# A 90 degree rotation of an 8192 x 8192 fp32 matrix: macro tiles of 512 rows with 4 MB stores in place of 1024 rows with 2 MB stores

## The chip, the cores and the metric

The kernel runs on one core of a Trainium2 chip. The metric is the time of one execution on the device in microseconds (us). The kernel before has a median of 1267.76 us over two runs (1267.45 and 1268.06).

## The reference

The input `x` is an 8192 x 8192 fp32 matrix (268.44 MB), `k` is 1, and the output has the same size:

```python
def reference(x, k):
    return np.rot90(x, k)
```

With k = 1 the output is `out[i, j] = x[j, 8191 - i]`: a transpose, with the order of the output's rows reversed. Every element is read once and written once, and nothing is computed on it.

## The kernel before

**Tiling.** The matrix is cut into macro tiles of R = 1024 rows by W = 4096 columns. There are 16 of them; `macro_tiles` cuts the last in two of 512 rows (`LAST`). A macro tile goes through four stages, and `load` and `store` are its two halves.

**Load.** A macro tile's rows come in row tiles of 128 (the partitions), 4096 columns each: one DMA of 2 MB, 16 KB to a partition, issued on SP's queue (line 102) into a buffer `a` (two of them; in the first macro tile some of the loads borrow an output buffer). VectorE (DVE, line 108) then copies the row tile in eight chunks `ar` of 512 columns and reverses the order of the columns in each block of 128. Chunks come from a ring of 63 buffers of 2 KB, in the order (row tile, chunk). A buffer comes free when TensorE (PE) has made the last transpose that reads it, and DVE waits for that. SP issues a load as soon as the `a` buffer that it writes has been copied out.

**Transposes.** PE turns each 128 x 128 block (line 148) and writes it into a PSUM tile `pt` of 128 x 2048 fp32, of which there are two. A PSUM tile takes 16 transposes.

**Evacuation and store.** ScalarE (ACT, line 169) copies a PSUM tile into the output buffer `ot`. There are three output buffers of 16 KB to a partition (F = 4096 elements), and each takes two PSUM tiles. ACT then issues the store on its own queue (line 177): 2 MB, 128 partitions of 16 KB, written to four output rows' pieces of 4 KB (1024 elements, the macro tile's rows). A macro tile has eight such stores. In the first macro tile two of them, and the last store of all, are issued as two stores of 1 MB (`S = PW`), which read 8 KB from a partition. The two macro tiles of 512 rows at the end write runs of 2 KB: their stores have 16 KB to a partition, in eight runs. `whole_reads` rewrites the read side of each DMA, so that what is contiguous in a partition is one read.

**Order.** Within an engine the order is that of the program. Load DMAs wait on SP only for DVE. Store DMAs wait on ACT only for ACT's copies. The two DMA queues, q1 (loads) and q10 (stores), share the core's 16 DMA engines. Transposes of a macro tile's first output are issued as each row tile comes in (`if i == 0 and ...`); all others follow once the whole macro tile is loaded. The next macro tile's loads go on meanwhile, as far as the chunk ring and the two `a` buffers allow. For the last two macro tiles the generators interleave loads and stores by hand.

Of the kernel before, what the change touches and what calls it, by code (L numbers as in the profile page):

```python
# [2 lines left out]

# [5 lines left out]

P = 128  # L10

R = 1024
RT = R // P
LAST = [4, 4]
W = 4096
CH = 512
F = 4096  # L20
FP = 2048


def whole_reads(nc):

    for fn in nc.m.functions:
        for block in fn.blocks:
            for n, ins in enumerate(block.instructions):
                if not isinstance(ins, mybir.InstDMACopy):
                    continue
                src = ins.ins[0]
                ap = [list(d) for d in src.ap]
                if len(ap) == 3 and ap[2][0] == 1 and ap[1][0] == ap[2][1]:
                    ap = [ap[0], [1, 1], [1, ap[1][1] * ap[2][1]]]
                    block.instructions[n] = copy.replace(  # L40
                        ins,
                        ins=[copy.replace(src, ap=ap)],
                        ant_dge_precooked=False,
                    )


def macro_tiles(N, M):

    tiles = [(r0, RT, c0) for r0 in range(0, N, R) for c0 in range(0, M, W)]
    r0, _, c0 = tiles.pop()  # L50
    for n in LAST:
        tiles.append((r0, n, c0))
        r0 += n * P
    return tiles


@with_exitstack
def kernel(
    ctx: ExitStack,
    tc: tile.TileContext,  # L60
    x: bass.AP,
    k: bass.AP,
    out: bass.AP,
):
    nc = tc.nc
    assert k == 1, f"only k=1 supported, got {k}"
    nc.at_finalize(whole_reads)

    N, M = x.shape
    dt = x.dtype  # L70

    consts = ctx.enter_context(tc.tile_pool(name="consts", bufs=1))
    ident = consts.tile([P, P], dt)
    make_identity(nc, ident)

    a_pool = ctx.enter_context(tc.tile_pool(name="a_pool", bufs=2))
    r_pool = ctx.enter_context(tc.tile_pool(name="r_pool", bufs=63))
    o_pool = ctx.enter_context(tc.tile_pool(name="o_pool", bufs=3))
    psum_pool = ctx.enter_context(
        tc.tile_pool(name="psum", bufs=2, space=bass.MemoryType.PSUM)  # L80
    )

    loads = 0

    def load(r0, rt, c0):

        nonlocal loads
        chunks = {}
        for t in range(rt):


            if loads < RT and loads % 5 >= 2:
                a = o_pool.tile([P, W], dt, tag="o")
            else:
                a = a_pool.tile([P, W], dt, tag="a")  # L100
            loads += 1
            nc.sync.dma_start(  # L102
                out=a[:], in_=x[r0 + t * P : r0 + (t + 1) * P, c0 : c0 + W]
            )
            yield chunks
            for j in range(W // CH):
                ar = r_pool.tile([P, CH // P, P], dt, tag="ar")
                nc.vector.tensor_copy(  # L108
                    out=ar[:],
                    in_=a[:, j * CH : (j + 1) * CH].rearrange(  # L110
                        "r (b m) -> r b m", m=P
                    )[:, :, ::-1],
                )
                chunks[t, j] = ar
            yield chunks

    def store(r0, rt, c0, chunks, end):

        rows = rt * P
        PW = 1
        while 2 * PW * rows <= FP:
            PW *= 2
        G = PW
        while 2 * G * rows <= F:
            G *= 2
        for i, g0 in enumerate(range(0, W // P, G)):  # L130
            if end and i % 2 == 0:
                ot = a_pool.tile([P, F], dt, tag="a")
            else:
                ot = o_pool.tile([P, F], dt, tag="o")
            o = ot[:, : G * rows].rearrange("m (g f) -> m g f", g=G)

            lead = r0 == 0 and c0 == 0 and i in (4, 6)
            S = PW if lead or (end and r0 + rows == N and g0 + G == W // P) else G  # L140


            ps = {}

            def transposes(t, ws):
                for w in ws:
                    g = g0 + w
                    nc.tensor.transpose(  # L148
                        ps[w // PW][:, PW - 1 - w % PW, t * P : (t + 1) * P],
                        chunks[t, g * P // CH][:, g % (CH // P), :],  # L150
                        ident,
                    )

            def psum_tile(h):
                pt = psum_pool.tile([P, FP], mybir.dt.float32, tag="ps")
                ps[h] = pt[:, : PW * rows].rearrange("m (g f) -> m g f", g=PW)

            if i == 0 and (rt == RT or r0 + rows < N):
                for h in range(G // PW):
                    psum_tile(h)  # L160
                for t in range(rt):
                    transposes(t, range(G))
            for h in range(0, G, PW):
                if h // PW not in ps:
                    psum_tile(h // PW)
                    for w in range(h, h + PW):
                        for t in range(rt):
                            transposes(t, [w])
                nc.scalar.copy(o[:, G - PW - h : G - h, :], ps[h // PW])  # L169

                done = h + PW
                if done % S == 0:
                    top = M - c0 - (g0 + done) * P
                    dst = out[top : top + S * P, r0 : r0 + rows].rearrange(
                        "(g m) f -> m g f", g=S
                    )
                    nc.scalar.dma_start(  # L177
                        out=dst, in_=o[:, G - done : G - done + S, :]
                    )
            yield  # L180

    tiles = macro_tiles(N, M)
    *most, before_last, last = tiles
    for m in most:
        *_, chunks = load(*m)
        for _ in store(*m, chunks, False):
            pass


    *_, chunks = load(*before_last)  # L190
    outputs = store(*before_last, chunks, True)
    rows = load(*last)
    for _ in range(2 * last[1] - 1):
        next(rows)
    next(outputs)
    chunks = next(rows)
    for _ in outputs:
        pass
    for _ in store(*last, chunks, True):
        pass  # L200


# [1 line left out]
_INS = ['x', 'k']  # L204
_OUTS = [((8192, 8192), 'float32')]

_NUMBERS = {'k': 1}


# [26 lines left out]
```

## Time and profile before

| What | Value |
|---|---|
| median of two runs | 1267.76 us |
| the profiled execution's span | 1266.1 us |
| PE busy | 718.2 us (57%), 4096 transposes |
| ACT busy | 466.7 us (37%), 256 copies of 1869 ns |
| DVE busy | 355.4 us (28%), 1024 copies of 421 ns |
| DMA | 537.55 MB, mean 425 GB/s |
| loads | 128 of 2 MB, median 16.8 us from issue to landing |
| stores | 125 of 2 MB, median 25.5 us; 6 of 1 MB, 27.3 us |
| TensorE clock, mean granted | 0.762 |

The page gives the profiled execution's own span; the median of the runs is 1.7 us above it. "Busy" is the time in which an engine had an instruction at work. A queue's line gives its packets, its megabytes and the time that its packets took as a share of the 16 DMA engines' time: two queues at 50% each leave no DMA engine free. A packet here is what is read from or written to one partition in one go; each DMA adds 16 very small ones (the lines' "under 512 B").

### The profile page before, as it was taken

Reading aid. Unit: us, or ns where it says so; the run is one execution under the profiler, and the core shown is the slowest. Engines: PE = TensorE matmul, PEld = TensorE weight load, DVE = VectorE, ACT = ScalarE, POOL = GpSimd, SP = SyncE. Lnnn points to the kernel's source line nnn. Section 1 sums busy time; section 2 is a strip of 40 time slices with the busy share of each in tenths; the row PEclk is TensorE's granted clock in tenths of the full one; section 3 lists DMA queues with packets and bytes.
Section 4 is the critical chain, followed back from the end, with each engine's and each line's share of the span. In section 5 each row is a group of like instructions: output and inputs, shape, how many; then the busy total and the mean of one; then the engine's idle time right before and its main releaser. Section 6 shows DMA issues by size and latency. Waiting matters only on the chain.

```text
span 1266.1 us, 10392 instructions
## 1 busy us (share of the span) xinstructions
PE 718.2 (57%) x4096; PEld 678.6 (54%) x4096; DVE 355.4 (28%) x1024; ACT 466.7 (37%) x257; POOL 0.7 (0%) x6
## 2 busy tenths in 40 slices
PE   1554565556656665556555665555655656556673
PEld 1543455555555555456554655555655655556562
DVE  4423223222232223222232223322232222322210
ACT  0432433433333333343334333343333433343363
POOL 0000000000000000000000000000000000000000
PEclk9977877777776777867778678677686686776797
DMA  9999999999999999999999999999999999999997
GB/s 399 426 428 430 428 429 427 430 429 429 429 429 429 430 428 427 430 429 430 428 430 428 429 429 428 430 428 428 430 430 428 429 429 428 428 428 428 427 399 328
DMA packets 37345, 537.55 MB, mean 425 GB/s; under 512 B 4144, under 2 KB 4144, under 8 KB 4144
## 3 DMA queue, kind: packets, MB, share of 16 engines
q10 hardware_dynamic: 18864, 268.44, 50.0%
q1 hardware_dynamic: 18432, 268.44, 49.7%
q8 instruction: 32, 0.52, 0.2%
q14 instruction: 17, 0.14, 0.0%
HBM read 268.44 MB, written 268.44 MB: 424 GB/s over the span
## 4 chain that ended last, share of the span: by engine, by line
DMA 82%; ACT 14%; PE 1%; issue 1%; ACTq 1%; DVE 0%; SPq 0%
DMA out_dram<-ot 79%; ACT ot L169 14%; DMA a<-in_x_dram 3%; PE pt L148 1%; ACTq L177 0%; DVE ar L108 0%; ACTq L169 0%; SPq L102 0%
## 5 line engine op out<-in xcount | busy, mean ns | idle before, releaser
L148 PE MATMUL pt<-ident,ar 128*128 128x128 f32 x4096 | 718.2, 356 | 528.0 <-ACT ot L169 487.6
L148 PEld LDWEIGHTS pt<-ident,ar 128*128 128x128 f32 x4096 | 678.6, 191 | 567.4 <-ACT ot L169 521.4
L169 ACT COPY ot<-pt 128x2048 f32<-128x2048 f32 x256 | 465.4, 1869 | 756.7 <-DMA out_dram<-ot 727.0
L108 DVE COPY ar<-a 128x512 f32<-128x512 f32 x1024 | 355.4, 421 | 861.1 <-DMA a<-in_x_dram 524.0
L169 ACT ACT_TABLE_LOAD x1 | 1.3, 1283 | 25.5 <-DVE ar L108 25.5
masks.py:199 POOL TENSOR_SCALAR_AFFINE_SELECT ident<-ident 128x128 f32<-128x128 f32 x1 | 0.3, 292 | 0.1
masks.py:197 POOL MEMSET ident<- 128x128 f32 x1 | 0.2, 204 | 0.3 <-POOLq L217 0.3
L217 POOL MEMSET const-bfloat16-1.0<- 128x1 bf16 x1 | 0.1, 102 | 0.0
L217 POOL MEMSET const-uint8-127<- 128x1 uint8 x1 | 0.1, 102 | 0.0
L217 POOL MEMSET const-float32-0.0<- 128x1 f32 x1 | 0.1, 99 | 0.2 <-issue 0.2
L217 POOL MEMSET const-float32-1.0<- 128x1 f32 x1 | 0.1, 99 | 0.0
## 6 DMA issues: line engine op xcount, KB each, us to landing
a<-in_x_dram SPq DMA_DIRECT2D x128, 2048.0 KB, 16.8
out_dram<-ot ACTq DMA_DIRECT2D x125, 2048.0 KB, 25.5
out_dram<-ot ACTq DMA_DIRECT2D x6, 1024.0 KB, 27.3
```

Of the source, the lines that this page charges most:

```text
L108: nc.vector.tensor_copy(out=ar[:], in_=a[:, j * CH : (j + 1) * CH].rearrange("r (b m) -> r b m", m=P)[:, :, ::-1],)
L148: nc.tensor.transpose(ps[w // PW][:, PW - 1 - w % PW, t * P : (t + 1) * P], chunks[t, g * P // CH][:, g % (CH // P), :], ident,)
L169: nc.scalar.copy(o[:, G - PW - h : G - h, :], ps[h // PW])
L217: nc = _bacc.Bacc("TRN2", target_bir_lowering=False, num_devices=1)
```

## The change

The macro tile has 512 rows instead of 1024, so there are 32 of them, each with four loads. F becomes 8192: an output buffer has 32 KB to a partition and takes four PSUM tiles, so a macro tile has two stores of 4 MB. Each reads 32 KB from a partition and writes it in 16 runs of 2 KB. The number of output buffers stays three. The chunk ring has 36 buffers instead of 63; a macro tile has 32 chunks. The special cases go: no loads into output buffers at the start, no split stores, no half macro tile at the end, no transposes ahead of the macro tile's last load other than by the plain loop order, and no interleaving of the last two macro tiles.

```diff
-R = 1024
+R = 512
 RT = R // P
-LAST = [4, 4]
 W = 4096
 CH = 512
-F = 4096
+F = 8192
 FP = 2048
...
-    r_pool = ctx.enter_context(tc.tile_pool(name="r_pool", bufs=63))
+    r_pool = ctx.enter_context(tc.tile_pool(name="r_pool", bufs=36))
...
+    PW = FP // R
+    G = F // R
+    for r0, c0 in [(r0, c0) for r0 in range(0, N, R) for c0 in range(0, M, W)]:
         chunks = {}
+        for t in range(RT):
+            a = a_pool.tile([P, W], dt, tag="a")
+            nc.sync.dma_start(out=a[:], in_=x[r0 + t * P : r0 + (t + 1) * P, c0 : c0 + W])
             for j in range(W // CH):
                 ar = r_pool.tile([P, CH // P, P], dt, tag="ar")
                 nc.vector.tensor_copy(
...
                 chunks[t, j] = ar
+        for g0 in range(0, W // P, G):
+            o = o_pool.tile([P, G, R], dt, tag="o")
             for h in range(0, G, PW):
+                pt = psum_pool.tile([P, PW, R], mybir.dt.float32, tag="ps")
+                for w in range(PW):
+                    g = g0 + h + w
+                    for t in range(RT):
+                        nc.tensor.transpose(
+                            pt[:, PW - 1 - w, t * P : (t + 1) * P],
+                            chunks[t, g * P // CH][:, g % (CH // P), :],
+                            ident,
+                        )
+                nc.scalar.copy(o[:, G - PW - h : G - h, :], pt[:])
+            top = M - c0 - (g0 + G) * P
+            nc.scalar.dma_start(
+                out=out[top : top + G * P, r0 : r0 + R].rearrange(
+                    "(g m) f -> m g f", g=G
+                ),
+                in_=o[:],
+            )
```

With R = 512, `PW` is 4 and `G` is 16. PSUM tile number h of a macro tile (0 to 7) reads exactly the chunks (0,h), (1,h), (2,h) and (3,h).

More of the change, by code (lines that the diff above doesn't have):

```diff
@@ L44, in whole_reads @@
                     )
[L47 to L54, printed above, removed]
 @with_exitstack
@@ L81 @@
     )
-    loads = 0
-    def load(r0, rt, c0):
-        nonlocal loads
+    PW = FP // R
+    G = F // R
+    for r0, c0 in [(r0, c0) for r0 in range(0, N, R) for c0 in range(0, M, W)]:
         chunks = {}
[L94 to L105, printed above, removed]
+        for t in range(RT):
+            a = a_pool.tile([P, W], dt, tag="a")
+            nc.sync.dma_start(out=a[:], in_=x[r0 + t * P : r0 + (t + 1) * P, c0 : c0 + W])
             for j in range(W // CH):
@@ L114, in load @@
                 chunks[t, j] = ar
[L115 to L162, printed above, removed]
-            for h in range(0, G, PW):
[L164 to L200, printed above, removed]
+        for g0 in range(0, W // P, G):
+            o = o_pool.tile([P, G, R], dt, tag="o")
+            for h in range(0, G, PW):
+                pt = psum_pool.tile([P, PW, R], mybir.dt.float32, tag="ps")
[15 more added lines that the diff above has]
+            )
```

## The prediction

> **What bounds the kernel now.** I read the page's slices and queues first.
>
> ```profile
> DMA  9999999999999999999999999999999999999997
> q10 hardware_dynamic: 18864, 268.44, 50.0%
> q1 hardware_dynamic: 18432, 268.44, 49.7%
> DMA out_dram<-ot 79%; ACT ot L169 14%; DMA a<-in_x_dram 3%; PE pt L148 1%; ACTq L177 0%; DVE ar L108 0%; ACTq L169 0%; SPq L102 0%
> ```
>
> The DMA engines are full from first to last slice, half with loads and half with stores, and the chain that ended last is stores. Then the waits, ACT's and DVE's:
>
> ```profile
> ACT ot L169 <- DMA out_dram<-ot: 727.0, 118, 11.0
> DVE ar L108 <- DMA a<-in_x_dram: 524.0, 82, 10.2
> ```
>
> Both engines wait for transfers, so only what changes the DMA engines' work or leaves them idle counts. From 600 to 640 us they move 428 GB/s with a share of 1.01: 2,097,152 bytes take 4.9 us (the first row tiles land at 8.02, 12.89 and 17.78 us, 4.89 apart). The whole 536.9 MB would take 1253 us; the other 13 us of the span are start and end.
>
> **Price one: the shape of a store.** At the end the two macro tiles of 512 rows already write 2 KB runs, with loads over. The queue view from 1222 to 1250 us:
>
> ```profile
> DMA packets 809, 11.71 MB, mean 418 GB/s; under 512 B 94, under 2 KB 94, under 8 KB 94
> q10 hardware_dynamic: 807, 11.68, 100.3%
> ```
>
> Full engines, 418 GB/s: 2.4% slower than 428. I take that for all 268.44 MB stored: 626.5 us becomes 641.5, +15 us. Ends: nothing (a store of 4 KB runs alone is shown nowhere, so the 2.4% may come from storing without loads; and one 32 KB read replaces two of 16 KB), and twice it, since no row shows 32 KB reads. One 4 MB store is 10.0 us of all engines, a macro tile 4 x 4.9 + 2 x 10.0 = 39.6 us, and 32 of them 1268 us.
>
> **Price two: how the queues share.** The 1 MB stores of the first macro tile read 8 KB from a partition. The queue views from 92 to 97 us and from 600 to 640 us:
>
> ```profile
> q1 hardware_dynamic: 102, 1.49, 69.7%
> q10 hardware_dynamic: 103, 0.71, 33.8%
> ...
> q10 hardware_dynamic: 590, 8.62, 50.7%
> q1 hardware_dynamic: 584, 8.49, 49.7%
> ```
>
> In both the queues take turns packet by packet: 103 to 102 and 590 to 584. With 8 KB against 16 KB, stores get a third of the time; with equal packets, half. So a 32 KB store packet beside a 16 KB load packet should give stores 2/3 and loads 1/3 while both have work: a load then takes 14.7 us instead of 9.8, and stores run off early. I take this; the other end is 1:1 as now.
>
> The Trainium skill's page "DMA: Bandwidth & Descriptors" (section "SWDGE vs HWDGE vs iDMA") says that a packet, the boundary at which an engine changes queues, is preferably at most 4096 B. By that the length of a read would not matter, the share would stay 1:1, and the sum would be that of the first rival below; the row from 92 to 97 us, where 8 KB and 16 KB packets alternate, speaks against it. The page "SBUF — State Buffer" (section "The DMA setup-cost knee") asks for the largest single transfer, at about 2 us fixed for each; 64 fewer stores would by that estimate save up to 128 us. The steady share of 1.01 shows no such gaps to save.
>
> **Price three: when transfers may start.** The zero is the moment at which a macro tile's fourth load lands. Primes mark the next macro tile's loads, 0' to 3'.
>
> Durations: a landed load's first chunk reaches PE 0.55 us later (8.02 to 8.56), eight chunk copies take 2.77. PE after a pause is slow, then fast; transposes in one microsecond, PEclk third from the end:
>
> ```profile
> 618.00:619.00 1.00, 1.00 (x7) 1.00 (x6) 0.50 1.04 442
> 1216.00:1217.00 1.00, 1.00 (x12) 1.00 (x11) 1.00 0.58 246
> ```
>
> So 0.147 us each cold (the mean of some 6.8), for about 4.8 us, then 0.11 (32 in 3.5 us). ACT takes 1.87 for a PSUM tile. A lone load needs 7.28 us from issue (0.74) to landing, 2.4 more than its 4.89 of data; I put 1.0 ahead of the data and 1.4 behind.
>
> Schedule: PSUM tile 0 has three transposes that need not wait; the other 13, cold, with the last one's drain, end at 2.9, tile 1 at 5.2, tile 2 at 7.2, tile 3 at 9.0. From tile 2 on the two PSUM buffers tie PE to ACT, which copies tile 3 until 11.0. **First store:** issued 11.0, moving at 12.0. Tiles 4 to 7 go on at ACT's pace: PE ends tile 7 at 17.2, **second store** issued 19.2. The 0.55 us issue is counted.
>
> Loads have a new tie. With 36 chunk buffers chunk (0',7) takes the buffer of (0,3), which PE frees at the end of tile 3, and (1',3) that of (0,7), freed at the end of tile 7. DVE is in order, and SP issues load 2' only when load 0' is copied out, 3' when 1' is. So 2' is issued at 9.5 at the earliest and 3' at 19.1; behind the waiting copy stand DVE's later chunks, and behind the waiting issue SP's later loads. Now DVE also waits for PE (337.1 us in all), but two further loads and the store backlog keep the engines full; that cover is now thinner.
>
> One cycle with shares 2:1: both stores, 20.0 us of work, run beside loads from 12.0 to 42.0. Loads 2' and 3' take 29.4 at a third of the rate, less three times what 2' got alone ahead of 12.0. If 2' starts at 10.5, load 3' is through at 36.9 and lands at 38.3; if at 11.9, at 42.5. Stores are thus over 3.7 us after that landing or 0.5 before it. Then loads 0'' and 1'' are alone, at full rate, and through at 11.8 or 9.0 of the next cycle, while 2'' starts no earlier than 10.5 (and 3.8 plus 1.4 after 0'' is through). In turn the engines stand idle some 0 to 0.3 and 1.5 us: about 0.7 per cycle. A cycle is 39.6 + 0.7 = 40.3.
>
> **Start and end.** Only two loads fly at first; the fourth lands at 23.0 (22.7 before). Idle there: 1.7 ahead of the first byte, 0.3 for the third load, 1.8 in the first cycle (loads 0' and 1' through at 8.7). End: after the last load no backlog is left but 0 to 2.5 us of stores, so the engines idle about 10 us until 12.0, then 20.0 of stores, then 2.4. The kernel before covers this with its half macro tiles.
>
> Removed: the split stores, borrowed buffers and interleaving cost nothing by themselves; their cover is what start and end lose. DVE, ACT and PE do the same 1024 copies, 256 copies and 4096 transposes. 64 store issues instead of 131 save some 36 us of ACT's queue, hidden by its wait of 727.0. Issues took 0.55 us until many 2 KB descriptors were outstanding at the end, then up to 3.63. At 19.2 such a stall delays nothing but the next macro tile's copies, 20 us off; at 11.0 it would push tiles 4 to 7, and load 3' to 23.2, against a start between 22 and 27 anyway.
>
> **Sum:** 1268 + 1.7 + 0.3 + 1.8 + 30 x 0.7 + 10 + 2.4 = 1305 us of span, and 1.7 from span to median: about 1306 us, 3% slower.
>
> **Rivals.**
> (1) *Not slower by 2%: equal shares.* If 32 KB reads don't shift the turns, loads get half, the load queue always has a next load (9.8 us each against starts at 10.5 and 20.1), and a store backlog of some 11 us covers the pause until 12.0, at the end too. Idle is some 5 us in all: 1268 + 5 + 2.4 + 1.7 = 1277, or 1262 if 2 KB runs cost nothing beside loads. It decides wherever the share of stores beside loads is below about 55%. For it: no row has 32 KB packets. Against: 102 to 103. 0.22.
> (2) *Shares 2:1, but stores cost as now:* 15 us off, with less idle 1279 to 1291. 0.12.
> (3) *More stalls:* PE cold all through a burst (2.35 us a PSUM tile against ACT's 1.87) and first issues of 3.6 us each add about 0.5 us to a cycle: 1306 + 16 or + 32, up to 1338. 0.13.
> (4) *Faster than 1242:* needs over 435 GB/s throughout; only longer packets could bring it, and no slice is above 430. 0.02.
> My forecast has the remaining 0.51, within 1294 to 1320.
>
> **Range and chances.** The low end takes in part of the first rival, 1268; the high end the third, 1332. Within 2% (1242 to 1293, about what a measurement of this kernel can tell from no change) lie rivals one and two: 0.34. Slower 0.64, faster 0.02.
>
> **What would show it.** In the changed profile: steady queue views with equal packets but stores at twice the loads' time while both run; loads landing some 15 to 25 us after issue; the DMA row below 1.0 once per cycle, just ahead of a first store; cycles of about 40.3 us; some 418 GB/s when stores run alone, an idle pause near 10 us before the last two stores. I would be wrong if the shares are equal, if 32 KB reads are cheaper or dearer than 2.4%, or if the idle pause per cycle is not 0.7 us, since each tenth of it is 3 us.

## The result, and the profile after

The changed kernel takes 1424.1 us (two runs, 1423.56 and 1424.63) against 1267.8: a ratio of 1.123, with a 95% interval of 1.120 to 1.127. The prediction was 1306 us, with 1332 as the upper end. The direction was right, the size was not: the loss is 156 us where 38 were forecast.

From the page of the changed kernel, its slices, queues and chain:

```profile
DMA  9999989999999999999999999999999999999997
GB/s 351 367 390 365 392 348 391 398 354 391 382 387 392 371 389 368 376 389 365 381 363 399 390 361 389 361 399 387 381 391 380 380 387 365 385 365 394 386 391 314
q10 hardware_dynamic: 9216, 268.44, 49.8%
q1 hardware_dynamic: 18432, 268.44, 47.2%
DMA 80%; DVE 10%; PE 5%; ACT 2%; issue 1%; DVEq 0%; ACTq 0%; SPq 0%
```

The row "DMA" looks like that of the kernel before: full. The row below it does not: no slice is above 399 GB/s, where most slices of the kernel before had 427 to 430. **Engines that are full and slow at once** are the finding of this case. The queue lines turn it into time. Before, stores took 50.0% and loads 49.7% of 1266.1 us: 633 and 629. Now stores take 49.8% of 1422.8, 708 us, and loads 47.2%, 672. The same bytes cost the engines 118 us more, and the time in which engines had nothing to do rose from 4 us to some 43. The two together are the 157 us by which the span grew.

The chain changed sides: it was stores, and is now loads. So did the waits:

```profile
DVE ar L82 <- DMA a<-in_x_dram: 979.3, 117, 19.1
ACT o L101 <- PE pt L96: 917.6, 129, 37.8
...
DVE ar L82 <- PE pt L96: 55.6, 11, 11.9
```

ACT no longer waits for an output buffer. DVE waits for loads, and PE and ACT wait behind it. The third line is the new tie between chunk buffers and loads for which the prediction has a schedule: it is met eleven times in all.

The turns of the queues, from 628 to 632 us:

```profile
q10 hardware_dynamic: 35, 1.15, 72.2%
q1 hardware_dynamic: 32, 0.49, 28.8%
```

Equal packets, and stores take two and a half times the loads' time. From the timeline, VectorE's copies, which start as each load lands:

```profile
648.07 2.77 DVE L82 COPY ar<-a 128x512 f32<-128x512 f32 x8 [5.01 <-DMA a<-in_x_dram]
652.92 2.78 DVE L82 COPY ar<-a 128x512 f32<-128x512 f32 x8 [2.08 <-DMA a<-in_x_dram]
659.01 2.77 DVE L82 COPY ar<-a 128x512 f32<-128x512 f32 x8 [3.31 <-DMA a<-in_x_dram]
663.84 2.77 DVE L82 COPY ar<-a 128x512 f32<-128x512 f32 x8 [2.06 <-DMA a<-in_x_dram]
685.68 2.77 DVE L82 COPY ar<-a 128x512 f32<-128x512 f32 x8 [19.07 <-DMA a<-in_x_dram]
```

A macro tile's fourth load lands at 648.07, the next one's at 685.68. Between them three loads come quickly, 4.8 to 6.1 us apart, almost all of it before the next store's first packet at 662.25, and the fourth takes 22 us beside the stores. In the cycle before that one, three loads in a row took some 15 us each. The cycles are uneven, as forecast, but from the first macro tile's fourth load (25.93) to the last one's (1387.39) they average 43.9 us, not 40.3.

### The profile page after: what moved, and what is told of

Read it like the earlier page. It is cut to its first block, busy times and chain, and to the rows that moved or that the text cites. A ratio compares the mean times of both kernels' runs of the same rounds, so it can differ in the third digit from the quotient of the medians.

```text
span 1422.8 us, 10460 instructions
## 1 busy us (share of the span) xinstructions
PE 571.3 (40%) x4096; PEld 519.2 (36%) x4096; DVE 355.2 (25%) x1024; ACT 470.5 (33%) x257; POOL 0.7 (0%) x6
## 3 DMA queue, kind: packets, MB, share of 16 engines
q10 hardware_dynamic: 9216, 268.44, 49.8%
q1 hardware_dynamic: 18432, 268.44, 47.2%
## 4 chain that ended last, share of the span: by engine, by line
DMA 80%; DVE 10%; PE 5%; ACT 2%; issue 1%; DVEq 0%; ACTq 0%; SPq 0%
DMA a<-in_x_dram 80%; DVE ar L82 10%; PE pt L96 5%; ACT o L101 2%; DVEq L82 0%; ACTq L103 0%; SPq L79 0%; ACTq L101 0%
## 5 line engine op out<-in xcount | busy, mean ns | idle before, releaser
L96 PE MATMUL pt<-ident,ar 128*128 128x128 f32 x4096 | 571.3, 302 | 833.8 <-DVE ar L82 796.9
L96 PEld LDWEIGHTS pt<-ident,ar 128*128 128x128 f32 x4096 | 519.2, 156 | 885.7 <-DVE ar L82 806.1
L101 ACT COPY o<-pt 128x2048 f32<-128x2048 f32 x256 | 469.2, 1871 | 935.8 <-PE pt L96 917.6
```

What stands on the lines that cost most here:

```text
L96: nc.tensor.transpose(pt[:, PW - 1 - w, t * P : (t + 1) * P], chunks[t, g * P // CH][:, g % (CH // P), :], ident,)
L101: nc.scalar.copy(o[:, G - PW - h : G - h, :], pt[:])
```

## The experiments

Three theories stood at the start. **A:** the 32 KB store packets take two turns' time of three and starve the loads. **B:** 2 KB runs beside loads slow the packets. **C:** large transfers let the engines drift apart.

### Equal packets: the same store read in two pieces

```diff
-                    ap = [ap[0], [1, 1], [1, ap[1][1] * ap[2][1]]]
+                    n_read = ap[1][1] * ap[2][1]
+                    cut = min(n_read, 4096)
+                    ap = [ap[0], [cut, n_read // cut], [1, cut]]
```

> The changed kernel with one edit: the 32 KB that a 4 MB store reads from a partition is cut into two reads of 16 KB; the transfer, its 2 KB runs, the buffers and the order stay. Theory A (a 32 KB store packet takes two thirds of the engines beside 16 KB load packets, and the starved loads stretch the cycle): shares go back to 1:1 and the time to some 1275 to 1295 us. Theory B (2 KB runs written beside loads slow the packets themselves, whatever is read in one go): stays at 1390 to 1425 us, with store packets still some 11% above their undisturbed length. Theory C (few large transfers let the 16 DMA engines drift apart, so that each load lands with its slowest engine): stays above 1360 us too, though with equal packets.

Measured: 1341.2 us, ratio 1.057 (1.056 to 1.059). From its page:

```profile
q10 hardware_dynamic: 17408, 268.44, 50.9%
q1 hardware_dynamic: 18432, 268.44, 48.4%
```

The turns are equal again and 83 us are gone, so theory A holds for about half of the loss. The span is 79 us shorter: 46 of it were time in packets, and some 34 time in which engines had nothing to do. But 50.9% and 48.4% of 1343.5 us are still 1334 us of packets, 72 more than in the kernel before. Something else lengthens them.

### Smaller stores, and the price of 2 KB runs

```diff
-F = 8192
+F = 4096
...
-    o_pool = ctx.enter_context(tc.tile_pool(name="o_pool", bufs=3))
+    o_pool = ctx.enter_context(tc.tile_pool(name="o_pool", bufs=6))
```

> The changed kernel with stores of 2 MB: 16 KB to a partition in eight 2 KB runs, and six output buffers of 16 KB in place of three of 32 KB. Theory A: equal packets, 1270 to 1295 us. Theory B: 1390 to 1425 us. Theory C: smaller and more transfers, so faster than the same kernel with 4 MB stores read in 16 KB pieces, near 1290 us.

Measured: 1285.4 us, ratio 1.014 (1.013 to 1.016). The other way to the same store is the kernel before with 512 rows:

```diff
-R = 1024
+R = 512
 RT = R // P
-LAST = [4, 4]
+LAST = [4]
```

> The kernel before with macro tiles of 512 rows: its 2 MB stores read 16 KB and write eight 2 KB runs throughout, with its three output buffers, 63 chunks and its special start and end. It prices the 2 KB runs alone. Theory A: the price measured at the end of the kernel before at most, 1268 to 1285 us. Theory B: over 1330 us.

Measured: 1284.4 us, ratio 1.014 (1.013 to 1.016). Two kernels with different buffers, starts and ends agree. Halving the runs to 2 KB, with 16 KB to a partition, costs 17 to 18 us; the prediction's row had said 15. Theory B in its plain form is dead. Between the 1341 of the store read in two pieces and these 1285 lie only the size of the transfer (and with it the count of runs and how far apart they lie) and the number of output buffers. That leaves theory C, or something in the shape of a 4 MB store.

### Shapes of transfers by themselves

This kernel moves data and rotates nothing: the output holds constants, and small copies keep the phases apart.

```diff
+    for n, run, g in PHASES:
+        if n:
+            loads(n)
+        if run:
+            stores(run, g)
+        barrier()
```

> Transfers alone, nothing rotated: the output holds constants. Thirteen phases kept apart by small copies: eight loads; then stores alone of 16.8 MB in four shapes (16 KB read into 4 KB runs, 16 KB into 2 KB, 32 KB into 2 KB, 32 KB into 4 KB); then the same four beside loads; then those four again. Theory A: stores alone run at 415 to 430 GB/s in every shape, and beside loads the two 32 KB shapes give stores twice the loads' time while the sum stays near 425 GB/s. Theory B: both shapes with 2 KB runs fall to 375 to 400 GB/s beside loads, those with 4 KB runs do not. Theory D (a 32 KB packet beside 16 KB packets itself costs rate): both 32 KB shapes fall, whatever their runs.

From the windows of that kernel (the last two columns are the DMA engines' share and GB/s); stores alone, in the order 16 KB into 4 KB runs, 16 into 2, 32 into 2, 32 into 4:

```profile
88.00:126.00 38.00, 1.56 (x12) 0.00 (x0) 1.00 1.01 428
129.00:167.00 38.00, 1.56 (x12) 0.00 (x0) 1.00 1.00 414
170.00:220.00 50.00, 2.18 (x16) 0.00 (x0) 1.00 0.99 391
223.00:260.00 37.00, 1.56 (x12) 0.00 (x0) 1.00 0.99 423
```

and beside loads, in the same order:

```profile
262.00:302.00 40.00, 0.00 (x0) 0.00 (x0) 1.00 1.01 432
331.00:395.00 64.00, 0.00 (x0) 0.00 (x0) 1.00 0.99 407
416.00:480.00 64.00, 0.46 (x3) 0.00 (x0) 1.00 0.99 384
486.00:540.00 54.00, 0.46 (x3) 0.00 (x0) 1.00 1.00 418
```

The third shape, that of the changed kernel, is slow with nothing else running: neither loads nor starved buffers are needed. The fourth reads 32 KB as well and is not slow, so theory D of the expectation falls. In the third the packet records of the first store follow a pattern of four: an engine's eight packets take about 1470, 1340, 1250 and 1270 ns in turn, twice over (means over the 16 packets that run at the same time, one on each engine). At the first rows of the four no engine is under 1341 ns, at the last two none over 1347. In the fourth shape all take 1228. All engines are slow at the same rows, so an engine's own drift (theory C) does not explain it; it points to the addresses. Loads beside this shape are slowed too: from 430 to 470 us a load packet takes 650 ns on average, from 490 to 530 us, beside the fourth shape, 618.

The packets alternate here as well, and the longer ones take the time. In the queue view from 430 to 470 us, with the third shape, and from 490 to 530 us, with the fourth:

```profile
q10 hardware_dynamic: 353, 9.99, 67.2%
q1 hardware_dynamic: 359, 5.21, 32.4%
...
q10 hardware_dynamic: 384, 11.01, 65.6%
q1 hardware_dynamic: 383, 5.75, 34.0%
```

### Many runs, or runs at bad distances

> Stores alone from constant buffers, nothing rotated, in ten phases: (1) 32 KB read into 16 runs of 2 KB, 128 rows (4 MB) apart, as in the changed kernel, which took 1359 ns a packet, 391 GB/s; (2) the same with the 16 runs in adjacent rows; (3) 48 KB into 16 runs of 3 KB; (4) 32 KB into 32 runs of 1 KB; (5) 16 KB into 16 runs of 1 KB; (6) like (1), but read in two pieces of 16 KB; (7) 8 KB into 4 runs of 2 KB; (8) like (1), with each transfer waited for; (9) 16 KB into 8 runs of 2 KB in adjacent rows; (10) 32 KB into 8 runs of 4 KB, read in two pieces. Theory F (the engines lose rate when a transfer has 16 or more runs to a partition, wherever they go): 1, 2, 3, 5, 6 and 8 are all some 8% below 415 GB/s, 4 more. Theory G (runs 4 MB apart in HBM collide from 16 on): 2 and 9 are at 414 GB/s or better, the far ones with 16 runs are slow. Theory H (a 32 KB read with many runs is what is slow): 6 and 5 run at full rate, 1, 2 and 8 do not.

Some of its transfers were issued in another order than their phases, so it is read transfer by transfer, from the packet records. Sixteen far runs of 2 KB: 365 to 400 GB/s. Sixteen runs in adjacent rows: 404 to 420. Sixteen far runs of 3 KB: 423 and 425. Sixteen far runs of 1 KB: some 340 to 395. Thirty-two: some 240 to 285. Sixteen far runs of 2 KB read in two pieces: 366 to 395. Four far runs of 2 KB: 415; eight in adjacent rows: 415 to 422. So the count of runs (theory F) is not it, nor the length of the read (theory H).

Three more transfers of the slow shape are not slow: 415, 417 and 420 GB/s, with most packets at 1247 ns. Before each of them a store into 4 KB runs had left the 16 engines out of step, so that their first packets start over 2.3 to 2.5 us. The next transfer of the same shape starts on all engines within 0.15 us, and the long packets are back (400 GB/s). So the loss seems to need engines that go through the same steps at the same time. No run varied that by itself, and it was not followed into the whole kernel.

Theory G is left, and was tested by moving the rows alone:

```diff
+                dst = out[top : top + g * pitch, r0 : r0 + 512].rearrange(
+                    "(g m) f -> m g f", m=pitch
+                )[lo : lo + P]
```

> Stores of 2 KB runs alone from constant buffers, nothing rotated, each phase from idle engines, six stores each (eight in phase 5): (1) 32 KB read into 16 runs 128 rows (4 MB) apart; (2) 16 runs 136 rows (4.25 MB) apart; (3) 16 runs in adjacent rows; (4) 24 KB into 12 runs 128 rows apart; (5) 16 KB into 8 runs 256 rows (8 MB) apart; (6) as 1, read in two pieces; (7) as 2, read in two pieces. Theory G (runs 4 MB apart collide in HBM from a certain count on): 1 and 6 at 365 to 395 GB/s; 2, 3 and 7 at 405 to 420; 4 between; 5 at 414, or near 390 if it is the spread of addresses and not the count of runs that matters. Theory F (the count of runs in a transfer, wherever they go): 1, 2, 3, 6 and 7 all at 365 to 395.

Its windows, phases 1 to 7 in order:

```profile
20.00:88.00 68.00, 0.00 (x0) 0.00 (x0) 1.00 1.00 370
91.00:151.00 60.00, 0.00 (x0) 0.00 (x0) 1.00 0.98 411
153.00:215.00 62.00, 0.00 (x0) 0.00 (x0) 1.00 1.00 406
218.00:268.00 50.00, 0.00 (x0) 0.00 (x0) 1.00 1.00 377
271.00:313.00 42.00, 0.00 (x0) 0.00 (x0) 1.00 0.99 393
316.00:384.00 68.00, 0.00 (x0) 0.00 (x0) 1.00 0.99 366
387.00:446.00 59.00, 0.00 (x0) 0.00 (x0) 1.00 1.01 422
```

Sixteen runs 128 rows apart: 370 GB/s (366 read in two pieces), 1414 ns a packet. The same runs 136 rows apart: 411 and 422, with packets of a flat 1247 ns (the first of these two windows runs past the end of its stores; by their packets they run at 421). Sixteen runs in adjacent rows: 406. Twelve runs 128 rows apart: 377. Eight runs, harmless 128 rows apart (414 in the kernel of shapes), fall to 393 when they are 256 rows apart. So the distance between a partition's runs changes the rate, and 2 KB runs in steps of 4 or 8 MB are slow once there are enough of them. No single rule comes out of these rows: 16 runs of 3 KB at the same 4 MB show no loss. This loss is called a collision below; what happens in the memory no run shows. The DMA share stays at 0.98 to 1.01 throughout, at 366 GB/s as at 422: **a lengthened packet counts as busy time from end to end.**

The Trainium skill's page "DMA: Bandwidth & Descriptors" (section "Latency and other measured facts") has an entry on row pitches of large powers of two, which says that copies at a pitch of 4 MiB from partition to partition ran at half their rate and that a padding of 4 KiB restored it. Here the 4 MB lie between the runs of one partition, and neighbouring partitions are one row (32 KB) apart. The loss is smaller, 370 against 411 to 422, and a padding of 8 rows restores the rate.

### The same in the whole kernel

```diff
-                    "(g m) f -> m g f", g=G
+                    "(m g) f -> m g f", g=G
```

The 16 runs of a partition now go to adjacent rows; only the place of the rows changes.

> The changed kernel with one edit: a partition's 16 runs of 2 KB go to adjacent rows of the output instead of rows 128 apart, so the output holds the right elements in a wrong order of rows. Reads of 32 KB, transfers, buffers and waits stay. Theory G: store packets return to about 1250 ns, and what remains is what the shares 2:1 cost: 1295 to 1330 us, where the prediction put the changed kernel. Theory F, or a cost that comes with 32 KB packets: stays at 1390 to 1425 us.

Measured: 1357.9 us, ratio 1.072 (1.071 to 1.074): 66 us less than the changed kernel, but above the 1295 to 1330 expected. By the shares of its page (48.8% and 49.1% of 1350.2 us), stores take 659 us (708 in the changed kernel), loads 663 (672), and the rest is some 28. The stores are cured for the most part: a mean store packet is 1286 ns in the trace, against 1383 in the changed kernel and the 1247 of the padded rows. The loads are not. With both edits, reads cut in two and runs adjacent:

> The changed kernel with both edits: stores read in 16 KB pieces (equal packets) and their runs in adjacent rows (the output's rows in a wrong order). Theory G: 1275 to 1295 us, as with 2 MB stores; the shares and the collisions are then all of the loss above the price of 2 KB runs. Theory F: 1330 to 1345 us, no better than with the reads cut alone.

Measured: 1295.2 us, ratio 1.022 (1.021 to 1.024), the upper edge of what theory G expected. So the 32 KB reads, with their unequal turns, cost 63 us without most of the collisions (1295 to 1358) and 83 with them (1341 to 1424).

The time in packets, by the shares of each page times its span, in us:

| Kernel | Stores | Loads | The rest |
|---|---|---|---|
| before | 633 | 629 | 4 |
| changed | 708 | 672 | 43 |
| changed, reads cut in two | 684 | 650 | 9 |
| changed, runs in adjacent rows | 659 | 663 | 28 |
| changed, both | 652 | 636 | 5 |
| changed, stores of 2 MB | 641 | 635 | 6 |

Of the 118 us by which packets grew, either edit alone takes back 46 or 58, and both together 92.

### What did not help

Reads cut in four pieces, so that loads get two thirds of the time:

```diff
-                    cut = min(n_read, 4096)
+                    cut = min(n_read, 2048)
```

> The changed kernel with each 4 MB store's 32 KB cut into four reads of 8 KB, so that beside loads a store gets one third of the engines instead of two thirds; runs and transfers stay. Theory A, shares alone: at most the 1341 us of 16 KB reads, and no idle engines ahead of the first store of a cycle. Theory C or F (4 MB transfers in 2 KB runs lengthen packets themselves): 1325 to 1360 us, no return to 1285.

Measured: 1331.3 us, ratio 1.048 (1.043 to 1.053). Favouring loads gains ten more. Its packets still take 1333 us, and ACT is held up in a new way: issuing a store, 0.55 us in the changed kernel, takes 10.9 us here at the median and up to 20.7, and ACT's copies stand behind it. The chain that ended last runs for 49% through ACT's issues. ACT also waits for output buffers again (263 us). Then more chunk buffers, paid for with an output buffer:

```diff
-    r_pool = ctx.enter_context(tc.tile_pool(name="r_pool", bufs=36))
-    o_pool = ctx.enter_context(tc.tile_pool(name="o_pool", bufs=3))
+    r_pool = ctx.enter_context(tc.tile_pool(name="r_pool", bufs=52))
+    o_pool = ctx.enter_context(tc.tile_pool(name="o_pool", bufs=2))
```

> The changed kernel with 52 chunk buffers in place of 36, paid for with two output buffers instead of three. By the prediction the third load of a macro tile could start only when the macro tile before had given up its chunks; 52 loosen that tie by half a macro tile. If the tie makes the idle pause of the prediction, up to 20 us are gained (about 1400 us). If loads are late because stores take two turns' time of three and their packets are long, nothing is gained: 1415 to 1435 us, or more where two output buffers make ACT wait.

Measured: 1456.9 us, ratio 1.149 (1.147 to 1.151), above the 1400 and the 1415 to 1435 us expected. The packets take 1418 us, 38 more than in the changed kernel; why was not looked into. The run does not show what looser chunks are worth by themselves. Four load buffers, paid for in the same way:

```diff
-    a_pool = ctx.enter_context(tc.tile_pool(name="a_pool", bufs=2))
+    a_pool = ctx.enter_context(tc.tile_pool(name="a_pool", bufs=4))
```

> The changed kernel with four load buffers in place of two, paid for with two output buffers instead of three. With more loads queued the engines should not fall idle: by the sum of packets the changed kernel's engines are idle for 44 us of its 1423, and most of that should go (1380 to 1400 us), while the lengthened packets (110 us) stay. If time falls below 1340, the long packets too came from loads that are too few in flight.

Its four times lie between 1428.7 and 1476.6 us, too far apart for a ratio; none is faster than the changed kernel. Both edits also took an output buffer, so neither isolates the load side. No version beat the kernel before.

## Why the prediction was wrong, point by point

**What bounds it: right.** The kernel before is at the rate of its DMA engines. No engine's own work set the end, but for the kernel with reads cut in four, where ACT's issues did.

**Price one, the shape of a store: the step that failed.** It said "one 4 MB store is 10.0 us of all engines, a macro tile 4 x 4.9 + 2 x 10.0 = 39.6 us, and 32 of them 1268 us". By the page's shares the packets took 708 + 672 = 1380 us, 112 more; that is nearly the whole miss of 118 us in span (1422.8 against 1305). Stores took 708 us in place of 641.5, and the loads, which the sum left at 4.9 us each (627 in all), 672. The row behind it, 418 GB/s at the end of the kernel before, was true of what it showed: 2 KB runs cost 17 to 18 us where 15 were put down. But it had eight runs to a partition, and the change has sixteen. Twice the price, the prediction's upper bound for this term, was 30 us. By the runs two things made the packets longer: the distance between a partition's runs (58 us, by moving them to adjacent rows) and the 32 KB read beside loads (46 us, by cutting it; a 32 KB read into 4 KB runs is not slow by itself, 423 GB/s). With both edits some 25 us are left above the kernel before. The kernel before had no row with sixteen runs. A bound drawn from the nearest shape does not hold when the pattern of addresses changes.

**Price two, the turns: right.** Packets alternate, and stores take 67 to 72% of the time beside loads. It was called from five microseconds of the old trace in which 8 KB and 16 KB packets alternated. Its effect was set too low: 63 to 83 us by the runs, where the prediction had some 30 us of pauses in it. The 32 KB packets cost more than idle engines; in the kernel with adjacent runs the loads' own packets are still 663 us in place of 629.

**Price three, the schedule: right where it can be read.** The last macro tile's fourth load lands at 1387.39; its stores are issued at 1398.84 and 1407.07, 11.5 and 19.7 us later, against 11.0 and 19.2. The cycles do alternate: from fourth load to fourth load they take 32 to 42 and 49 to 54 us in turn. The idle time in all was put at 37 us and is about 43 by the shares. That they are so close is in part luck: the end has less of it than forecast, and the cycles have more, some 1.1 us each in place of 0.7. And the tie of load 2' to the chunk ring binds only eleven times, because loads are later than it. The pauses stand elsewhere; in the windows from 650 to 654 us:

```profile
650.00:652.00 2.00, 2.00 (x11) 2.00 (x10) 0.84 (x3) 0.38 (x1) 0.00 (x0) 0.50 0.60 180
652.00:654.00 2.00, 2.00 (x12) 2.00 (x11) 1.07 (x4) 1.49 (x1) 0.00 (x0) 0.50 0.83 303
```

The fourth load has landed at 648.07. The next macro tile's first load is nearly through, and its second waits until DVE has copied the fourth load's buffer out, at 650.84; its first packets start at 651.8. What holds it is the two load buffers, not the chunk ring.

**Start and end: right in kind.** The first macro tile's fourth load lands at 25.93, not 23.0. After the last load the engines stand idle, but for some 6 us instead of 10:

```profile
1390.00:1395.00 5.00, 4.90 (x38) 4.53 (x37) 0.17 (x1) 3.85 (x3) 0.00 (x0) 0.86 0.74 308
1395.00:1400.00 5.00, 4.89 (x42) 4.54 (x43) 0.00 (x0) 4.12 (x3) 0.00 (x0) 1.00 0.01 3
```

**Rivals.** Equal shares (1277) was wrong as to the changed kernel; with equal packets by a cut read it is 1341, and with 2 MB stores 1285. "More stalls" named PE's clock and ACT's issues, and neither made the loss: a store's issue takes 0.55 us at the median and 0.65 at most, and the last macro tile's stores come half a microsecond later than the schedule has them. One count of the working is off, and nothing in the sum rests on it: from 131 stores to 64 is 67 fewer, not 64. That the same bytes could take the engines 112 us longer was no rival at all. It stood only in the upper bound of price one and in the last sentence, as "32 KB reads are cheaper or dearer than 2.4%".

**The loss in steps**, each the difference of two medians: 2 KB runs 18 us (1267.4 to 1285.4), 4 MB transfers with equal packets 56 (to 1341.2), 32 KB reads 83 (to 1424.1). Moving the runs to adjacent rows takes back 46 of the second step, or 66 where the reads are whole.

**What stays open.** Why steps of 4 MB are slow was not looked into; only the dependence on distance is shown. Why the loads' packets lengthen in whole kernels with 32 KB stores, even with adjacent runs, is known in part. A load that starts on idle engines has long first packets (1.0 to 1.4 us instead of 0.61 at one such start in the changed kernel's trace). In the trace of the kernel with adjacent runs the first 16 packets of a load, about one for each engine, take 728 ns on average, and the others 634; in the kernel before it is 617 and 613. So the first packets hold some 14 of the 34 us, and the rest is not explained. And 136 rows between runs, the clean cure in the transfers by themselves, was not tried in the whole kernel: the output has no room for the gaps.

## What to carry to other kernels

Price a transfer by its addresses as well as by its bytes and runs: before one store is made wider, look at how far apart its runs land, and take a large power of two as a risk that only a run can price. Read GB/s beside the DMA share, since full engines can be slow. And compare the packet lengths of queues that share the engines: here the queue with the longer packet took the time, and the other one's consumers waited.

## What was not expected

- Sixteen 2 KB runs 128 rows (4 MB) apart store at 370 GB/s; 136 rows apart, at 411 to 422. Sixteen runs of 3 KB at the same 128 rows show no loss (423 to 425), and neither do three transfers of 2 KB runs whose engines were out of step (415 to 420).
- A 32 KB read is not slow by itself: into 4 KB runs it stores at 423 GB/s alone.
- Thirty-two runs of 1 KB fall to some 240 to 285 GB/s.
- With its reads cut in four, a 4 MB store takes ACT 10.9 us to issue at the median, in place of 0.55.
